# Two boundaries of a decoder layer: the first two tiles of an output product's tail by all tokens instead of by halves

## The chip, the core and the metric

The kernel runs on one core of one Trainium2 chip. The metric is device time in microseconds: the median of several executions of the whole program. Engines are named as in the profile: PE (TensorE) multiplies matrices, PEld is its load of weights, DVE (VectorE) and ACT (ScalarE) work elementwise, POOL is GpSimd, SP issues most DMAs. Each engine works its queue in the order in which instructions were put there, and waits where an input is missing.

## The reference

One decoder layer over 512 tokens of width 1024, in float32, with three residual steps:

```python
h = rms_norm(x, ffn1_pre_g);  x = x + 0.5 * rms_norm(swiglu(h, ffn1_w_in, ffn1_w_out), ffn1_post_g)
h = rms_norm(x, mix_pre_g);   proj = h @ w_mix_in           # q, k, v, u
mixed = concat([dilated_attention(q, k, v), s5_mixer(u, ...)]) @ w_mix_out
x = x + rms_norm(mixed, mix_post_g)
h = rms_norm(x, ffn2_pre_g);  x = x + 0.5 * rms_norm(swiglu(h, ffn2_w_in, ffn2_w_out), ffn2_post_g)

def rms_norm(x, g):   # over the 1024 channels of a token
    return x * rsqrt(mean(x * x) + 1e-6) * g
```

Between two of these steps a *boundary* lies: the output product of the step before has to be finished, its rows normalised and added to `x`, and the new `x`, with the gain of the next norm, goes into the next step's first products. The factor of that next norm is applied later, to the products.

## The kernel before

Activations lie transposed: 128 channels of a tile on the partitions, the 512 tokens along the free dimension; a 1024-wide activation is eight such tiles (`KD` = 8). A token's sum over channels is thus a sum over partitions and over tiles, and is made by matmuls with a column of ones.

Products run in a pair format: an operand is split into a rounded high part and the low rest (`split`: ACT makes `xh`, DVE makes `xl` from `x` and `xh`), and `mm3` issues three matmuls, high by high, high by low, low by high, in this order. A tile of the tail (`NT` = 4 blocks of the inner dimension) is therefore 4 x 3 = 12 matmuls. All matmuls that the boundary issues go through `mm`, which pins them in the order of the program.

`boundary` is called twice: after the first feed-forward step (its output is `y`) and after the mixer (`ymix`). Most of the output product has been made before; what is left is the tail, the last four blocks. The work goes by halves of the tokens (`HT` = 256), so that the norm of the first half can be worked out while TensorE makes the second half:

- `product(h, m)`: the 12 matmuls of output tile m on half h, into half of a PSUM bank; tiles 0 to 5 share a bank by pairs, 6 and 7 have one each.
- `gather(h, m, n, b)` (L287): DVE adds n tiles from PSUM into `y`.
- `squares(h, m, n, eng)` (L293, L296): ACT squares n tiles of `y` and, except for m = 0, which goes straight into `acc[h]`, an addition into `acc[h]` follows, on POOL (`G`) or DVE (`V`). The two columns of `acc[h]` hold even and odd tiles.
- `fold` (L168): POOL adds the two columns of `acc`.
- `post[h][0]`, made by `rstd`: the fold (for the first half), four matmuls `st` with the ones, `nv` on DVE (L190), a power on POOL (L192). `post[h][1]`: four matmuls `rp` that spread the factor over the partitions.
- `prep(h, k)`: L302 and L304 on DVE (scale `y` by the gain and the factor, add to `x`), then `split` for the next step (`xh` on ACT L151, `xl` on DVE L152), and the square of `x` for the next norm (L161, L163 on POOL).
- `begin(h, k)`: 12 matmuls of the next step's first products, into the banks `first`.

Tiles 0 and 1 of the first half come first, the first three blocks of both and then the last block of both, because the last block's input can be late. Then come tiles 2 to 7 of the first half, then the eight tiles of the second half. After tile 2 of the second half stands `post[0][0]`, after tile 3 `post[0][1]` and `prep(0, 0)`, `prep(0, 1)`. Behind the tail the loop over k alternates `prep(0, k)` and `begin(0, k)`; `post[1]` is worked in at k = 2 and 4; then the same for the second half, with the next norm's sums at k = 3 and 6.

The order on an engine is made by a scheduler ahead of time, by a model of readiness and the order of the program. What passes through `fix` is *pinned*: it is issued behind everything that the program has given to that engine before. POOL's additions in `squares` and, where `fixp=fx` is given, POOL's fold and power are pinned. DVE's gathers and the preps up to k = 5 are not.

```python
                (fix if eng is V else fx)(eng.tensor_tensor(out=ac, in0=ac, in1=t, op=ALU.add))   # squares
                self.fold(acc, nc.gpsimd, fixp or fix)                                            # rstd, sums
```

## Time and profile before

| what | value |
|---|---|
| median of 3 runs | 957.33 us (956.88 to 957.65) |
| the profiled execution | 957.78 us, its span 956.0 us |
| granted clock of TensorE, mean | 0.997 |
| first boundary's tail products | 354.66 to 378.13 us |
| its first products of the next step, up to the last spread | 378.13 to 402.40 us |
| second boundary's tail products | 552.54 to 576.60 us |
| its first products of the next step, up to the last spread | 576.60 to 600.90 us |

The span runs from the first to the last instruction. Rows of the timeline give start, length, engine, line, operation, the tile written and those read, shapes and a count, and in brackets how long the engine was idle before and what ended that. A row with a count above 1 is several instructions merged. Rows of the chain of waits give start, length and what the end of the program hung on in that time.

### The profile page before, as it was taken

The numbers are of one execution on the slowest core, as the hardware profiler recorded it, in microseconds if no ns is written. First come the engines' busy times: TensorE is split into PE (matmuls) and PEld (weight loads), VectorE is DVE, ScalarE is ACT, GpSimd is POOL, SyncE is SP. The second block draws the span as 40 slices with busy tenths as digits, with TensorE's granted clock in tenths as the row PEclk, the third lists the DMA queues.
The fourth block names the chain that finished last, engine by engine and source line by source line (L and its number), as shares of the span: only waits on it lengthen the run. The fifth ranks groups of instructions, "written<-read, shape, count | busy, mean of one in ns | idle before, by whom it ended". The sixth has DMA issues, their size and how long they took to land.

```text
span 956.0 us, 12871 instructions
## 1 busy us (share of the span) xinstructions
PE 942.2 (99%) x5082; PEld 789.3 (83%) x5082; DVE 528.3 (55%) x934; ACT 367.3 (38%) x610; POOL 223.5 (23%) x134
## 2 busy tenths in 40 slices
PE   9999999999999999999999999999999999999995
PEld 7888888888888889978777899888888888888884
DVE  6999213463256546758897659644135524453427
ACT  6354334352234233525646645543233222232312
POOL 0234222322223233500000034421112112223300
PEclk9999999999999999999999999999999999999998
DMA  8223334353334241292323420422232222323202
GB/s 264 90 99 109 102 110 138 125 177 103 106 114 132 67 154 45 90 232 81 121 71 126 147 90 1 131 79 99 88 111 89 93 105 89 110 88 132 88 1 89
DMA packets 38173, 102.48 MB, mean 107 GB/s; under 512 B 7616, under 2 KB 10944, under 8 KB 37568
## 3 DMA queue, kind: packets, MB, share of 16 engines
q1 hardware_dynamic: 36528, 98.02, 31.8%
q10 hardware_dynamic: 1584, 3.63, 1.1%
q8 instruction: 40, 0.66, 0.3%
q14 instruction: 21, 0.17, 0.1%
HBM read 94.03 MB, written 7.60 MB: 106 GB/s over the span
## 4 chain that ended last, share of the span: by engine, by line
PE 93%; DVE 3%; ACT 1%; issue 1%; DMA 1%; POOLq 0%; POOL 0%; ACTq 0%; DVEq 0%; SPq 0%
PE gu L129 47%; PE yo L129 20%; PE first L129 6%; PE yt L129 6%; PE prj L129 3%; PE prv L129 2%; PE mo L129 2%; PE st L129 1%; PE ys L129 1%; PE gl L129 1%; PE pt L832 1%; PE sc L129 1%; PE pv L129 1%; PE rp L129 0%; ACT whi L102 0%
## 5 line engine op out<-in xcount | busy, mean ns | idle before, releaser
L104 POOL TENSOR_TENSOR wlo<-wraw,whi 128x1024 fp32r<-128x1024 f32 (+2 forms) x62 | 156.6, 2526 | 498.9 <-ACT whi L102 490.7
L102 ACT CAST whi<-wraw 128x1024 fp32r<-128x1024 f32 (+5 forms) x157 | 154.6, 990 | 303.5 <-PE gu L129 119.8
L129 PE MATMUL gu<-xh,whi 128*128 128x512 f32 x656 | 257.7, 393 | 0.0
L129 PE MATMUL gu<-xh,wlo 128*128 128x512 f32 x656 | 255.7, 390 | 0.5 <-DVE wlo L104 0.5
L129 PE MATMUL gu<-xl,whi 128*128 128x512 f32 x656 | 255.3, 389 | 0.0
L104 DVE TENSOR_TENSOR wlo<-wraw,whi 128x1024 fp32r<-128x1024 f32 (+5 forms) x95 | 115.9, 1226 | 121.7 <-ACT whi L102 121.4
L129 PEld LDWEIGHTS gu<-xh,wlo 128*128 128x128 f32 x656 | 123.1, 188 | 27.0 <-DVE wlo L104 1.0
L129 PEld LDWEIGHTS gu<-xh,whi 128*128 128x128 f32 x656 | 123.2, 188 | 25.3 <-issue 0.4
L129 PEld LDWEIGHTS gu<-xl,whi 128*128 128x128 f32 x656 | 123.2, 188 | 25.0
L402 DVE TENSOR_TENSOR ut<-gu,rs 128x512 f32<-128x512 f32 x41 | 28.2, 689 | 102.9 <-PE gu L129 102.9
L149 DVE TENSOR_TENSOR al<-ut,ah 128x512 fp32r<-128x512 f32 x44 | 65.7, 1494 | 25.4 <-ACT ah L148 25.4
L129 PE MATMUL yo<-ah,whi 128*128 128x512 f32 x144 | 56.0, 389 | 0.0
L129 PE MATMUL yo<-al,whi 128*128 128x512 f32 x144 | 56.0, 389 | 0.0
L129 PE MATMUL yo<-whi,ah 128*128 128x512 f32 x144 | 56.0, 389 | 0.0
L129 PE MATMUL yo<-wlo,ah 128*128 128x512 f32 x144 | 56.0, 389 | 0.0
L129 PE MATMUL yo<-whi,al 128*128 128x512 f32 x144 | 56.0, 389 | 0.0
L129 PE MATMUL yo<-ah,wlo 128*128 128x512 f32 x144 | 56.0, 389 | 0.0
L400 DVE TENSOR_TENSOR gt<-gu,rs 128x512 f32<-128x512 f32 x41 | 28.2, 688 | 50.0 <-PE gu L129 50.0
L148 ACT CAST ah<-ut 128x512 fp32r<-128x512 f32 x44 | 27.3, 622 | 64.3 <-DVE ut L403 64.3
L129 PE MATMUL first<-xh,whi 128*128 128x256 f32 (+1 forms) x144 | 44.0, 306 | 0.2 <-ACT xh L151 0.2
L403 DVE TENSOR_TENSOR ut<-ut,gt 128x512 f32<-128x512 f32 x44 | 41.5, 946 | 4.1 <-ACT whi L102 0.5
L129 PE MATMUL first<-xl,whi 128*128 128x256 f32 (+1 forms) x144 | 43.5, 302 | 0.0
(194 smaller groups left out, 1410.2 us busy)
## 6 DMA issues: line engine op xcount, KB each, us to landing
wraw<-w2i SPq DMA_DIRECT2D x44, 512.0 KB, 3.5
wraw<-w1i SPq DMA_DIRECT2D x42, 512.0 KB, 3.5
wraw<-w2o SPq DMA_DIRECT2D x18, 512.0 KB, 3.4
wraw<-w1o SPq DMA_DIRECT2D x16, 448.0 KB, 3.4
wraw<-wmi SPq DMA_DIRECT2D x12, 512.0 KB, 3.6
x<-xT SPq DMA_DIRECT2D x8, 256.0 KB, 4.8
w1d<-w1s SPq DMA_DIRECT2D x8, 256.0 KB, 2.8
w2d<-zb SPq DMA_DIRECT2D x2, 1024.0 KB, 4.9
```

The lines of the kernel that those rows point to most:

```text
L102: fix(self.nc.scalar.copy(out=hi, in_=raw))
L104: fix(eng.tensor_tensor(out=lo, in0=raw, in1=hi.bitcast(F32), op=ALU.subtract))
L129: i = self.nc.tensor.matmul(*a, **k)
L148: fix(nc.scalar.copy(out=hi, in_=src))
L149: fix(nc.vector.tensor_tensor(out=lo, in0=src, in1=hi.bitcast(F32), op=ALU.subtract))
L400: nc.vector.tensor_tensor(out=gt, in0=o[f][0], in1=r, op=ALU.mult)
L402: nc.vector.tensor_tensor(out=ut, in0=o[f][1], in1=r, op=ALU.mult)
L403: nc.vector.tensor_tensor(out=ut, in0=ut, in1=gt, op=ALU.mult)
L832: self.fix(nc.tensor.transpose(b[i][:, o:o + P], sc[:, c:c + P], self.ident))
```

## The change

In `boundary`, tiles 0 and 1 of the tail are made on all 512 tokens, with their own bank each, at the start; the second half's loop begins with tile 2. The gathers of the two tiles are 512 wide, and their squares are taken for both halves at once. The calls of `post[0]` in the second half's loop stand behind tiles 4 and 5 instead of 2 and 3.

```diff
@@ -311,15 +311,16 @@
         V, G, fx = nc.vector, nc.gpsimd, self.fix
-        b2 = [self.bank("yt")[:, :HT] for _ in range(2)]
+        b2 = [self.bank("yt") for _ in range(2)]
         for ks in (range(NT - 1), (NT - 1,)):
             for m in range(2):
                 for k in ks:
                     th, tl = tail(k)
-                    self.mm3(b2[m], tw(0, m, k), tw(1, m, k), th[:, hs[0]], tl[:, hs[0]], k == 0, k == NT - 1)
+                    self.mm3(b2[m], tw(0, m, k), tw(1, m, k), th, tl, k == 0, k == NT - 1)
         for m in range(2):
-            gather(0, m, 1, b2[m].unsqueeze(1))
-        squares(0, 0, 2, V)
+            nc.vector.tensor_tensor(out=y(m), in0=b2[m], in1=y(m), op=ALU.add)
+        for h in range(2):
+            squares(h, 0, 2, V)
         for m in range(2, KD):
             b = product(0, m)
             if m % 2 or m > 5:
@@ -327,7 +328,7 @@
                 gather(0, m, n, b)
                 squares(0, m, n, G if m == 2 else V)
         late = []
-        for m in range(KD):
+        for m in range(2, KD):
             b = product(1, m)
             if m % 2 or m > 5:
                 m1, n = (m - 1, 2) if m < 6 else (m, 1)
@@ -337,9 +338,9 @@
                     late.append(t)
                 if m == 5:
                     self.fold(acc[1], G, fx)
-            if m == 2:
+            if m == 4:
                 post[0][0](fixp=fx)
-            if m == 3:
+            if m == 5:
                 rr[0] = post[0][1]()
                 for k in range(2):
                     prep(0, k)
```

## The prediction

> **What bounds the kernel now.** I read the page first, then the busy time by stretches of the two boundaries, then the chain of waits through them, then the timeline of each engine around the places that the edit moves.

> ```profile
> span 956.0 us, 12871 instructions
> PE 942.2 (99%) x5082; PEld 789.3 (83%) x5082; DVE 528.3 (55%) x934; ACT 367.3 (38%) x610; POOL 223.5 (23%) x134
> 354.66:378.13 23.47, 23.47 (x203) 23.47 (x202) 11.78 (x23) 7.20 (x13) 7.42 (x6) 1.00 0.18 62
> 552.54:576.60 24.06, 23.73 (x203) 23.53 (x202) 14.10 (x26) 9.08 (x16) 7.49 (x7) 1.00 0.21 67
> ```

> The last two rows are the tail products of the first and of the second boundary; their columns are the stretch and its length, then the busy time of PE, PEld, DVE, ACT and POOL, the granted clock, and the DMA's share and rate. TensorE is busy in all of the first tail and misses 0.33 us in the second, at a granted clock of 1.00. So nothing but TensorE's own time can be saved there, and any wait of TensorE that the edit makes is added to the span one for one. Whether there is such a wait is the whole question.

> ```profile
> 333.06 21.76 PE yo L129 x96
> 354.82 15.55 PE yt L129 x132
> 372.67 5.46 PE yt L129 x48
> ...
> 553.81 0.04 issue
> 553.85 14.99 PE yt L129 x125
> 568.85 0.34 PE st L129 x4
> 569.18 1.52 PE yt L129 x12
> 570.70 0.45 PE rp L129 x4
> 571.15 5.46 PE yt L129 x48
> 576.61 4.32 PE first L129 x36
> ```

> These are pieces of the chain of waits (start, length, what). One 512-wide product costs 21.76 / 96 = 0.2267 us, a 256-wide one 15.55 / 132 = 0.1178 us. The order of TensorE around the row sums is to be seen too: products, `st` (sums of the first half's squares), one tile of 12 products, `rp` (the spread of the norm), four more tiles (48 products), then `first`, the next stage's products on the first half.

> **Wider tiles.** The edit takes 48 products of 256 away and puts 24 of 512 in: 48 x 0.1178 - 24 x 0.2267 = 0.21 us less in each boundary, 0.42 us in both. Of the tail's 192 products 144 stay as they are.

> **The start of the second boundary.** Here products wait for the gated SSM outputs (`so`).

> ```profile
> 552.54 0.99 PE L129 MATMUL yt<-so,tw 128*128 128x256 f32 x7
> 553.85 14.99 PE L129 MATMUL yt<-so,tw 128*128 128x256 f32 x125 [0.33 <-DVE so L152]
> 553.12 1.47 DVE L152 SCALAR_TENSOR_TENSOR so<-go,so 128x512 fp32r<-128x512 f32 x2
> ```

> The eighth product needs the low part of the third `so` tile; it would start at 552.54 + 7 x 0.1178 = 553.36 and starts at 553.85, a hole of 0.49 us. With 512-wide products the eighth is due at 552.54 + 7 x 0.2267 = 554.13, after the tile has come, and the last `so` tile (done at 553.12 + 1.47 = 554.59) is wanted only behind 18 products, at 556.6. The hole goes: 0.49 us less. The first boundary has no such hole.

> **The first row sums.** This is the step that I think decides. `post[0][0]` moves from behind tile 2 to behind tile 4 of the second half. It issues one fold of `acc[0]` on POOL (L168), four `st` products, `nv` on DVE and a power on POOL. The fold is pinned in program order (`fixp=fx`), behind whatever POOL got before it. Today the only tile pair of the second half ahead of it is (0, 1), and `squares` issues no addition for m = 0. After the edit the pair (2, 3) is ahead, whose `squares(1, 2, 2, G)` issues a pinned POOL addition of 128x512. So the fold stands in POOL's queue behind an addition whose input comes from products that TensorE has finished only one tile before. The `st` products need the fold, and all matmuls are pinned, so behind the waiting `st` stand product(1, 5), the spread and everything else.

> ```profile
> 558.99 0.69 DVE L287 TENSOR_TENSOR ymix<-yt,ymix 128x512 f32<-128x512 f32 x1 [2.26 <-PE yt L129]
> 559.77 0.63 ACT L293 ACTIVATE sq<-ymix 128x512 f32<-128x512 f32 x1 [2.38 <-DVE ymix L287]
> 560.48 1.28 POOL L296 TENSOR_TENSOR acc<-acc,sq 128x512 f32<-128x512 f32 x1 [1.78 <-ACT sq L293]
> 565.25 0.78 DVE L296 TENSOR_TENSOR acc<-acc,sq 128x256 f32<-128x256 f32 x2 [0.19 <-ACT sq L293]
> 566.12 0.74 POOL L168 TENSOR_TENSOR acc<-acc 128x256 f32<-128x256 f32 x1 [4.35 <-DVE acc L296]
> 567.47 0.69 DVE L287 TENSOR_TENSOR ymix<-yt,ymix 128x512 f32<-128x512 f32 x1 [1.43 <-PE yt L129]
> 568.57 0.53 PEld L129 LDWEIGHTS st<-ones,acc 128*128 128x128 f32 x4
> ```

> The first three rows are the same kind of pair (tiles 2 and 3 of the first half): from the gather's start to the POOL addition's start 560.48 - 558.99 = 1.49 us, the addition 1.28. The fold today starts 566.12 - 566.03 = 0.09 us after what it waits for and takes 0.74; TensorE picks up a finished input in about 0.04 us (553.81, where the DVE op before it in the chain ends, to 553.85). So `st` can load 1.49 + 1.28 + 0.09 + 0.74 + 0.04 = 3.64 us after the start of the gather of (2, 3). TensorE is ready for it one tile after that pair, and the last two rows show that distance for the pair (0, 1) today: 568.57 - 567.47 = 1.10 us. **The wait is 3.64 - 1.10 = 2.54 us in each boundary, 5.08 us in both.** Today's slack hides nothing of it: the fold ends at 566.86 and `st` comes at 568.57, 1.7 us of cover, and that cover is what the queue position takes away. Below and above: no wait if the fold were issued ahead of the addition, 2.54 as derived, and up to 0.19 more if the addition takes 1.47 as in a row below. I take 2.54.

> The chance to do better, that POOL overtakes, has no row in this trace. [...]

> **The spread to the first products.** `rp` ended at 571.15, and 48 products (5.46 us) lay between it and `first`. After the edit only tiles 6 and 7 lie there, 24 x 0.1178 = 2.83 us. In that time `prep(0, 0)` must deliver `xh` and `xl`.

> ```profile
> 571.35 0.86 DVE L302 SCALAR_TENSOR_TENSOR ymix<-ymix,sm,rp 128x256 f32<-128x256 f32 x2
> 572.13 1.85 DVE L304 TENSOR_TENSOR x<-ymix,x 128x256 f32<-128x256 f32 x2
> 573.91 0.47 DVE L302 SCALAR_TENSOR_TENSOR ymix<-ymix,sm,rp 128x256 f32<-128x256 f32 x1
> 574.30 0.48 DVE L152 SCALAR_TENSOR_TENSOR xl<-x,sm,xh 128x256 fp32r<-128x256 f32 x1
> 572.24 1.47 POOL L296 TENSOR_TENSOR acc<-acc,sq 128x512 f32<-128x512 f32 x1 [2.07 <-ACT sq L293]
> 572.58 0.51 ACT L151 ACTIVATE xh<-x,sm 128x256 fp32r<-128x256 f32 x1 [0.42 <-DVE x L304]
> 375.82 0.47 DVE L152 SCALAR_TENSOR_TENSOR xl<-x,sm,xh 128x256 fp32r<-128x256 f32 x1
> 576.91 0.41 DVE L287 TENSOR_TENSOR ymix<-yt,ymix 128x256 f32<-128x256 f32 x1
> ```

> The first `xl` is there at 574.30 + 0.48 = 574.78, 3.63 us after `rp` ended at 571.15 (in the first boundary at 376.29, 3.62 us after its `rp` ended at 372.67). The second `first` product needs it, at 2.83 + 0.12 = 2.95 us. With 0.04 us to pick it up: **0.72 us of wait in each boundary, 1.44 in both.** I expect the same order on DVE and the same POOL addition beside it, now that of the pair (4, 5), so the same 3.63. Bounds: if DVE's order puts the low part directly behind the long L304 (573.98), 0.40 us less; if two 256-wide gathers (0.41 each) slip in, 0.82 more. So 0.32 to 1.54.

> **The rest of the prepared half.** Behind the spread `first` stands 5.46 - 2.83 - 0.72 = 1.91 us nearer to `rp` than today, so later preps have less time.

> ```profile
> 574.69 0.41 DVE L304 TENSOR_TENSOR x<-ymix,x 128x256 f32<-128x256 f32 x1
> 575.91 0.68 DVE L287 TENSOR_TENSOR ymix<-yt,ymix 128x512 f32<-128x512 f32 x1
> 578.02 1.02 DVE L304 TENSOR_TENSOR x<-ymix,x 128x256 f32<-128x256 f32 x1
> 588.57 0.57 DVE L152 SCALAR_TENSOR_TENSOR xl<-x,sm,xh 128x256 fp32r<-128x256 f32 x1
> 585.58 10.08 PE first L129 x84
> ```

> The tightest place is the first `xl` of the second half: done at 589.14, that is 17.99 us behind `rp`, wanted today at 585.58 + 37 x 0.12 = 590.02 (18.87). After the edit it is wanted at 18.87 - 1.91 = 16.96. But DVE has less to do by then: the gather of (4, 5), 0.68, is done before `rp`, and one of the POOL additions that stretch an L304 is gone (1.02 against 0.41 where nothing is beside it, 0.61). 17.99 - 1.29 = 16.70, just in time. I take nothing; the other end, with no such saving, is 17.99 - 16.96 = 1.03 us per boundary. Weight loads, the SP queue, `late` and the second spread keep their places relative to `first`; the end of the boundary hangs on TensorE's own `rp` and moves with it.

> **The sum.** -0.42 - 0.49 + 5.08 + 1.44 = +5.6 us. Against the profiled execution (957.78 us, 956.0 of it span) that is 963.4; it lies 0.45 above the median of the three runs, 957.33, so I forecast **962.9 us** for the median.

> **The rivals.**
> 1. *Only the second wait comes*: the fold is not held, because it is issued ahead of the addition. -0.42 - 0.49 + 1.44 = +0.5, 957.9 us, within what can be told apart: the case on the other side. Place: POOL between tiles 3 and 4 of the second half; it decides if gather to `st` shrinks from 3.64 below 1.10 us. Against it: the pin and the order of the calls. 8%.
> 2. *Neither wait comes*: 957.33 - 0.91 = 956.4 us. It needs also the first `xl` within 2.95 us of `rp`; today it takes 3.63. 4%.
> 3. *Only the first wait comes*: DVE's order brings the low part in time. 962.9 - 1.44 = 961.5 us. 8%.
> 4. *DVE becomes the bound in the second half*: 1.03 us more in each boundary, 965.0 us. For it: a margin of only 0.26 us. 10%.
> 5. *The fold keeps DVE out as well.* The L304 rows show DVE standing still beside POOL: its second L304 ends at 573.98, 0.27 after the POOL addition's end at 573.71. After the edit a fold of 0.74 stands right behind that addition. If POOL holds on for both, `xl` comes 0.83 us later, 962.9 + 1.66 = 964.6 us. 5%. [...] A row speaks against a second op being waited out:

> ```profile
> 577.46 1.30 POOL L296 TENSOR_TENSOR acc<-acc,sq 128x512 f32<-128x512 f32 x1 [1.75 <-ACT sq L293]
> 578.85 0.80 POOL L168 TENSOR_TENSOR acc<-acc 128x256 f32<-128x256 f32 x1
> ```

> The L304 begun at 578.02 ended at 579.04, inside the fold that stood behind the addition: it got in between the two.

> **How the numbers follow.** Forecast 65%, rivals 8, 4, 8, 10 and 5%. The unknown costs alone give 957.33 - 0.91 + 5.08 + 2 x 0.32 = 962.1 to 957.33 - 0.91 + 5.08 + 2 x 1.54 = 964.6; with rival 3 below and 4 above, and some tenths for the scatter of the runs (956.88 to 957.65), **961.0 to 965.3**. Outside are rivals 1 and 2. A measurement of this kernel tells about 0.2%, 1.9 us, from no change: slower means above 959.2. Rivals 1 and 2 fall within: same 0.12; slower 0.85; faster 0.03 for something that I don't see.

> **What would show it.** Right: in both boundaries the POOL fold L168 directly behind an L296 addition, a hole of 2.5 us on TensorE ahead of `st` laid to that fold, a second of 0.7 us ahead of the second `first` product laid to `xl`, and no hole at 553.4. Wrong: a fold that starts before the (2, 3) addition of its half, or TensorE without a hole in the tail; then the sum falls to that of rival 1 or 2. A hole at the start of the second half of `first` is rival 4.

## The result, and the profile after

| | before | changed |
|---|---|---|
| median | 957.29 us (956.88 to 957.65, 4 runs) | 967.30 us (966.29 to 968.62, 4 runs) |
| ratio to before, 95% interval | | 1.0104 [1.0092, 1.0115] |
| profiled execution, its span | 957.78 us, 956.0 us | 966.29 us, 964.5 us |

The changed kernel is 10.0 us slower. The direction was forecast; the size was not: 5.6 us were forecast, and the time lies 2.0 us above the range.

The first fence is from the page of the changed kernel, the second from its waits of TensorE (total us, times, longest).

```profile
span 964.5 us, 12769 instructions
PE 942.9 (98%) x5034; PEld 787.6 (82%) x5034; DVE 526.0 (55%) x932; ACT 367.4 (38%) x610; POOL 227.1 (24%) x134
```

```profile
PE st L129 <- POOL acc L168: 4.2, 2, 2.1
PE first L129 <- DVE xl L152: 2.0, 4, 0.8
PE ys L129 <- issue: 1.8, 2, 0.9
```

TensorE is as busy as before (942.9 against 942.2 us, in a span 8.5 us longer), so the time went into waits. Two of the three rows are the forecast ones: `st` waits for POOL's fold once in each boundary, and `first` waits for `xl`. The third was not forecast; `ys` belongs to the mixer, between the two boundaries.

The chain of waits through the first boundary (start, length, what):

```profile
353.54 16.92 PE yt L129 x120
...
370.48 0.70 DVE y L287
...
371.27 0.64 ACT sq L293
...
371.98 1.26 POOL acc L296
373.24 0.69 POOL acc L168
...
373.98 0.61 PE st L129 x4
374.58 1.49 PE yt L129 x12
...
376.10 0.69 DVE y L287
376.79 0.78 DVE y L302 x2
377.57 1.77 DVE x L304 x2
379.34 0.33 DVE y L287
379.68 0.54 DVE xl L152
...
380.26 4.52 PE first L129 x35
```

Before, this chain held TensorE alone. Now it leaves TensorE twice. First from the gather of tiles (2, 3) over the square and POOL's addition to the fold, which starts the moment the addition ends. Then over DVE from the gather of (4, 5) to the first `xl`, with a gather (L287, 0.33) that stands ahead of `xl`.

To see where each microsecond went, I took the starts of TensorE's first row of each tile from the timeline, in this and every later profile, and their differences as stage lengths, in us:

| stage | before | changed | difference |
|---|---|---|---|
| start of the program, up to the first `rp` | 36.10 | 34.73 | -1.37 |
| first boundary: first `yt` to `st` | 15.55 | 20.60 | +5.05 |
| `st` to `rp` | 1.86 | 1.92 | +0.06 |
| `rp` to `first` | 5.90 | 3.27 | -2.63 |
| `first` to the next stage | 25.82 | 27.13 | +1.31 |
| *first boundary, sum* | 49.13 | 52.92 | +3.79 |
| `ys`, in the mixer | 11.76 | 13.03 | +1.27 |
| second boundary: first `yt` to `st` | 16.14 | 20.59 | +4.45 |
| `st` to `rp` | 1.86 | 3.20 | +1.34 |
| `rp` to `first` | 5.90 | 3.50 | -2.40 |
| `first` to the next stage | 25.83 | 27.08 | +1.25 |
| *second boundary, sum* | 49.73 | 54.37 | +4.64 |

The rest of the span differs by 0.2 us in all. The start is scatter: over the kernels below that leave it alone it lies between 34.5 and 36.1. So the boundaries cost 8.4 us, and `ys` 1.3.

The second boundary holds something that the first does not. Its chain:

```profile
577.05 0.63 PE st L129 x4
577.69 2.77 PE yt L129 x12
580.46 0.74 PE rp L129 x4
```

Twelve products took 2.77 us here and 1.49 in the first boundary, behind the same wait. Busy time by stretches (length, then PE, PEld, DVE, ACT, POOL with counts, granted clock, DMA share and rate), the first boundary in the first two rows and the second in the others:

```profile
369.29:372.70 3.41, 2.57 (x22) 2.36 (x21) 0.69 (x1) 0.63 (x1) 0.72 (x1) 1.00 0.00 0
372.70:376.11 3.41, 2.13 (x18) 2.13 (x19) 0.17 (x2) 0.00 (x0) 1.94 (x3) 1.00 0.02 5
574.09:577.50 3.41, 1.29 (x12) 1.09 (x11) 0.17 (x1) 0.63 (x1) 1.95 (x2) 1.00 0.00 0
577.50:580.91 3.41, 3.41 (x18) 3.41 (x18) 0.57 (x2) 0.00 (x0) 0.71 (x1) 0.50 0.00 0
580.91:584.32 3.41, 3.12 (x27) 2.92 (x26) 3.38 (x7) 1.86 (x4) 2.19 (x2) 1.00 0.03 7
```

The granted clock fell to 0.50 for 3.41 us behind the wait of the second boundary and stayed at 1.00 behind that of the first; why the stretches are cut at these times is told with e10. Against the first boundary's lengths the lower clock cost 3.20 - 1.92 + 3.50 - 3.27 = 1.51 us.

### The profile page after: what moved, and what is told of

Same layout as the page of the kernel before. It is cut to its first block, busy times and chain, and to the rows that moved or that the text cites. A ratio compares the mean times of both kernels' runs of the same rounds, so it can differ in the third digit from the quotient of the medians.

```text
span 964.5 us, 12769 instructions
## 1 busy us (share of the span) xinstructions
PE 942.9 (98%) x5034; PEld 787.6 (82%) x5034; DVE 526.0 (55%) x932; ACT 367.4 (38%) x610; POOL 227.1 (24%) x134
## 3 DMA queue, kind: packets, MB, share of 16 engines
q10 hardware_dynamic: 1584, 3.63, 1.1%
## 4 chain that ended last, share of the span: by engine, by line
PE 90%; DVE 5%; DMA 1%; issue 1%; ACT 1%; POOL 1%; POOLq 0%; DVEq 0%; ACTq 0%
PE gu L129 45%; PE yo L129 20%; PE yt L129 5%; PE first L129 5%; PE prj L129 3%; PE mo L129 2%; PE prv L129 2%; PE st L129 1%; PE ys L129 1%; PE gl L129 1%; DMA wraw<-w1i 1%; DVE wlo L104 1%; PE pt L833 1%; PE sc L129 1%; PE pv L129 1%
## 5 line engine op out<-in xcount | busy, mean ns | idle before, releaser
L129 PE MATMUL gu<-xh,whi 128*128 128x512 f32 x656 | 257.6, 393 | 0.0
L129 PE MATMUL gu<-xh,wlo 128*128 128x512 f32 x656 | 255.7, 390 | 0.5 <-DVE wlo L104 0.5
L129 PE MATMUL gu<-xl,whi 128*128 128x512 f32 x656 | 255.3, 389 | 0.0
L129 PEld LDWEIGHTS gu<-xh,wlo 128*128 128x128 f32 x656 | 123.1, 188 | 26.8 <-DVE wlo L104 1.0
L129 PEld LDWEIGHTS gu<-xh,whi 128*128 128x128 f32 x656 | 123.2, 188 | 25.3 <-issue 0.4
L129 PEld LDWEIGHTS gu<-xl,whi 128*128 128x128 f32 x656 | 123.2, 188 | 25.1
L149 DVE TENSOR_TENSOR al<-ut,ah 128x512 fp32r<-128x512 f32 x44 | 68.6, 1560 | 25.4 <-ACT ah L148 25.4
L129 PE MATMUL yo<-ah,whi 128*128 128x512 f32 x144 | 56.0, 389 | 0.0
L129 PE MATMUL yo<-al,whi 128*128 128x512 f32 x144 | 56.0, 389 | 0.0
L129 PE MATMUL yo<-whi,ah 128*128 128x512 f32 x144 | 56.0, 389 | 0.0
L129 PE MATMUL yo<-wlo,ah 128*128 128x512 f32 x144 | 56.0, 389 | 0.0
L129 PE MATMUL yo<-whi,al 128*128 128x512 f32 x144 | 56.0, 389 | 0.0
L129 PE MATMUL yo<-ah,wlo 128*128 128x512 f32 x144 | 56.0, 389 | 0.0
L129 PE MATMUL first<-xl,whi 128*128 128x256 f32 (+1 forms) x144 | 43.2, 300 | 2.0 <-DVE xl L152 2.0
L129 PE MATMUL first<-xh,whi 128*128 128x256 f32 (+1 forms) x144 | 43.2, 300 | 0.8 <-ACT xh L151 0.8
L129 PE MATMUL first<-xh,wlo 128*128 128x256 f32 (+1 forms) x144 | 42.4, 295 | 0.0
```

The lines of the kernel that those rows point to most:

```text
L129: i = self.nc.tensor.matmul(*a, **k)
L149: fix(nc.vector.tensor_tensor(out=lo, in0=src, in1=hi.bitcast(F32), op=ALU.subtract))
```

## The experiments

Each kernel is the changed kernel with the edit shown, unless another is named. The ratios are to runs of the kernel before beside it (medians 957.21, 957.14 and 956.82 us in the three groups of runs). In the expectations A is the theory that POOL's and DVE's queues make the waits and that TensorE, idle in them, then gets a lower clock; the theory called F is explained where it comes up, and the rivals B, C, D, G and H in the expectations that name them.

### The wait at `st`

**e1: the fold ahead of the second half.** It is issued before the loop, so that no addition stands ahead of it.

```diff
-        def sums(more=(), fix=lambda i: i, fixp=None):
+        def sums(more=(), fix=lambda i: i, fixp=None, fold=True):
-            if folded and not more:
+            if fold and folded and not more:
...
         late = []
+        self.fold(acc[0], G, fx)
         for m in range(2, KD):
...
-                post[0][0](fixp=fx)
+                post[0][0](fixp=fx, fold=False)
```

> The changed kernel with one difference: the fold of acc[0] is issued on POOL ahead of the second half's additions; st, nv and the power stay where the change put them. Theory A (POOL's order holds st, and the idle TensorE then gets a lower clock): st waits for nothing; the power, pinned behind the addition of tiles 2 and 3, comes 0.6 us late, so rp waits 0.6 us per boundary; the granted clock is back at 0.997; the wait at the second first product stays at 1.0. Time 957.3 - 0.9 + 2 x 0.6 + 2 x 1.2 = 960 us, between 959 and 961.5. Rival B (st waits for its late place and for gathers that come late, whatever POOL's order): st still waits over 2 us, time 966 to 968.

964.04 us (960.94 to 965.03), ratio 1.0067 [1.0053, 1.0081]. The chain of the first boundary:

```profile
371.64 1.28 POOL acc L296
372.92 0.69 POOL p L192
...
373.66 0.72 PE rp L129 x4
```

The wait at `st` is gone from both boundaries (first `yt` to `st` 18.33 us in place of 20.60). The power (L192), now the op behind the addition, comes late in place of the fold, and `rp` waits a little: `st` to `rp` is 2.29, against 1.86 where nothing is late. So POOL's order makes the wait. The time is 4 us above the 960 that A expected, though, and 2.5 above its range: `ys` took 15.69 us in this profile.

**e2: that addition on DVE.**

```diff
-                t = squares(1, m1, n, G if n == 2 else None)
+                t = squares(1, m1, n, (V if m1 == 2 else G) if n == 2 else None)
```

> The changed kernel with one difference: the addition of the squares of tiles 2 and 3 of the second half runs on DVE instead of POOL, so nothing stands ahead of the fold in POOL's queue. Theory A: no wait at st nor at rp, clock back at 0.997, what is left is the second wait of about 1.2 us per boundary. Time 957.3 - 0.9 + 2.4 = 958.8 us, between 957.8 and 960. Rival B: st still waits over 2 us, 966 to 968.

963.40 us (962.02 to 964.55), ratio 1.0065 [1.0052, 1.0077]. Both boundaries now take 50.58 us, with 18.33 to `st` and 1.85 from there to `rp`: no wait at `st`, none at `rp`, and no fall of the clock in either. The difference to the changed kernel, 20.60 - 18.33 = 2.27 us, is what the first wait costs in a boundary, lower clock not counted. The `xl` wait stayed (27.12). And again the time is above A, which expected 958.8, again by `ys`: 16.40 us.

**e3 and e10: work put into the wait, and behind it.** Twenty spare products of 128x256 into an unused bank stand ahead of `st` in e3, and behind it in e10.

```diff
             if m == 4:
+                fill = self.bank("idle")
+                for _ in range(20):
+                    self.mm(fill[:, :HT], lhsT=tw(0, 0, 0), rhs=tail(0)[0][:, hs[0]], start=True, stop=True)
                 post[0][0](fixp=fx)
```

> The changed kernel with 20 more matmuls of 128x256 into a spare bank directly ahead of st, work that nothing reads: they fill the wait (20 x 0.118 = 2.4 us) and take no time from anything else if st has to wait 2.5 us anyway. Theory A (the idle 2.3 us lowers TensorE's clock afterwards): the clock stays at 0.997 and the time falls by what the lower clock cost, to 964 us, between 963 and 965.5, with less spread between runs. Rival C (the surplus over the forecast has nothing to do with the clock): 967.3 as before, or slower.

> The changed kernel with the same 20 spare matmuls of 128x256, now behind st instead of ahead of it: TensorE idles through the wait as in the changed kernel and then has 2.4 us more to do, where the filler ahead of st filled the wait. Both kernels issue the same instructions. Theory A (an idle of 2.3 us lowers the granted clock for some us afterwards): slower than the kernel with the filler ahead by 2.4 us per boundary and by what the lower clock costs, 1 to 2 us where it falls: 965.0 + 4.7 + 2 to 4 = 972 to 974, granted clock 0.99 or below, windows behind st at 0.5 to 0.9. Rival C (no clock effect): 965.0 + 4.7 = 969.7 and the clock at 0.996.

e3: 964.98 us (963.82 to 966.18), ratio 1.0080 [1.0067, 1.0093]. e10: 972.44 us (970.83 to 973.07), ratio 1.0155 [1.0135, 1.0175]. Chains of the first boundary, e3 and then e10:

```profile
372.74 2.35 PE idle L129 x20
375.09 0.40 PE st L129 x4
375.50 1.50 PE yt L129 x12
```

```profile
374.30 0.61 PE st L129 x4
374.91 3.99 PE idle L129 x20
378.90 1.37 PE yt L129 x12
```

In e3 the 2.35 us of spare work cost nothing: `st` comes 20.68 us after the first `yt`, against 20.60 without them. They lie wholly within the wait. In e10 the same products cost their full time, and more, because they run at the lower clock: 3.99 us in place of 2.35. Stretches of e10:

```profile
374.00:376.00 2.00, 1.70 (x11) 1.70 (x12) 0.16 (x1) 0.00 (x0) 0.97 (x2) 0.76 0.03 8
376.00:378.00 2.00, 2.00 (x11) 2.00 (x11) 0.00 (x0) 0.00 (x0) 0.00 (x0) 0.50 0.00 0
378.00:380.00 2.00, 2.00 (x18) 2.00 (x18) 0.00 (x0) 0.00 (x0) 0.00 (x0) 0.89 0.00 0
```

In e3, where TensorE does not stand idle there, the boundaries' clock stayed at 1.00 (353 to 382 us and 555 to 586 us). So it was the idle stretch that the clock fell behind, and e3 is faster than the changed kernel though it does more work. e3 and e10 issue the same instructions, and only the order differs: 972.44 - 964.98 = 7.46 us between the medians, of which the 40 spare products at full clock explain 4.70. The other 2.8 come with the lower clock, in the median and not only in one profile: the four executions of e10 had mean granted clocks of 0.992 to 0.995, the six of e3 0.996 to 0.998.

Some of what decides whether the clock falls behind a wait can be read off the times at which it fell. e6, an experiment told below, has the same two waits, and its clock fell in both boundaries:

```profile
378.48:381.89 3.41, 3.41 (x17) 3.41 (x17) 0.85 (x2) 0.00 (x0) 0.72 (x1) 0.50 0.00 0
583.28:586.69 3.41, 3.41 (x19) 3.41 (x18) 1.98 (x4) 0.63 (x1) 0.81 (x2) 0.50 0.01 2
```

The two falls are 583.28 - 378.48 = 204.80 us apart, 60 x 3.413. e10's are as far apart (375.04 and 579.84). In the changed kernel the clock changed at 577.50 and 580.91, 3.41 us apart, and fell again at 956.38, when the products were done, 375.47 us or 110 x 3.413 later. So within each of these three profiles the times lie on a grid of 3.41 us, and the grid's place is not the same in all: 583.28 in e6 and 577.50 in the changed kernel are 5.78 us apart, 1.7 stretches. In the changed kernel the second wait (574.94 to 577.06) lies whole in one stretch, 574.09 to 577.50, and the next stretch is at half clock. The first wait (371.86 to 373.98) is cut by the line at 372.70 (577.50 less 60 stretches) into 0.84 and 1.28 us, and the clock stays. Four profiles have two such waits each, of 2.12 to 2.17 us: changed, e6, e10 and e12. In e6 and e10 each wait has 2.05 us or more within the one stretch ahead of a fall. In e12, where the clock is 0.60 from 376 to 378 us and 0.54 from 378 to 380, the fall began at about 376.4; the first wait (373.32 to 375.44) lies whole in the stretch ahead of it, and the second (576.62 to 578.79) is cut at about 577.8 and was followed by a clock of 1.00 (580 to 582). So six of the eight were followed by a fall, and the two that were not are the two that the grid cut into pieces of 1.3 us or less.

Other stretches agree with this. At the changed kernel's end one with 2.01 us of idle time (952.97 to 956.38) was followed by a fall. The waits of 2.25, 2.56 and 3.35 us in `ys` in e1, e4 and e2, told below, have matmuls of 35 ns behind them in place of 29; behind e8's wait of 1.57 us there they take 29. How much idle time it takes between 1.57 and 2.01 us is not shown. A fall in a boundary lasted one stretch, in e10's second boundary two; one stretch at half clock loses 3.41 / 2 = 1.7 us of work.

### The wait for `xl`, and DVE's order

**e4: the sums and the spread early.** `post[0][0]` directly behind tile 3's products and ahead of the gather of (2, 3); the spread and two preps behind tile 4.

```diff
             b = product(1, m)
+            if m == 3:
+                post[0][0](fixp=fx)
             if m % 2 or m > 5:
...
             if m == 4:
-                post[0][0](fixp=fx)
-            if m == 5:
                 rr[0] = post[0][1]()
```

> The wide tiles of the change, but the sums st and the fold are issued behind product 3 and ahead of the gather and the squares of tiles 2 and 3, the spread rp behind product 4, with three tiles left behind it. Theory A: the fold is done 2.2 us after the first half's last product and st comes after 2.8, no wait; behind rp lie 36 products, 4.2 us, more than the 3.7 that the first xl needs, no wait; what is left is the gain of wide tiles and of the hole at the start of the second boundary, -0.9 us: 956.4 us, between 955.9 and 957.2. Rival D (DVE is the bound of what follows, since TensorE comes 1.2 us earlier): waits at later first products, 957.5 to 959. Rival B: over 960.

959.64 us (955.57 to 962.40, 12 runs), ratio 1.0025 [1.0013, 1.0037]. The boundaries fell to 49.54 and 49.52 us. `st` no longer waits. A wait of 0.3 us is left in each boundary, at the third `first` tile, for its `xl`, which stands on DVE behind gathers and two L302 (26.17 in place of 25.82). A had expected 956.4. `ys` was 15.58 us in this profile, in which the mean granted clock was 0.995. Three of the twelve executions were at 0.995; the other nine, at 0.996 or 0.997, have a median of 959.2, so a fall of the clock is not all that keeps e4 above the kernel before.

**e9: that prep earlier.** On top of e4 and of the shift explained below, `prep(0, 2)` is called with the first two.

```diff
-                for k in range(2):
+                for k in range(3):
                     prep(0, k)
         for k in range(KD):
-            if k > 1:
+            if k > 2:
                 prep(0, k, fx if k > 5 else lambda i: i)
```

> The shifted kernel with the early sums and with prep(0, 2) called beside prep(0, 0) and prep(0, 1), so that DVE is given it ahead of the last gathers. In the early-sums kernel TensorE waits 0.8 us per boundary at the third first product for DVE's order (gathers of tiles 6 and 7 and two L302 ahead). If that order is the cause, the waits at first go from 1.6 us in all to under 0.6 and the time is about 1 us below that of the shifted early-sums kernel, 955.5; if DVE is simply full there, the wait moves to a later first product or to the second half's sums and the time stays.

960.92 us (959.83 to 961.69), ratio 1.0040 [1.0028, 1.0053]. `first` to the next stage is back at 25.83 us in both boundaries, as before the change; DVE's order was the cause. Against e7, which differs from it by this prep alone, the boundaries are 0.49 us shorter and the median 0.49 (960.92 against 961.41).

### The third place: `ys`

e1, e2 and e4, in which the wait at `st` is taken away, kept several microseconds that the boundaries did not hold. In their profiles they were in `ys`, 384 matmuls of about 30 ns with a load each. Its code is the same in all kernels. Chains of before, changed and e2, in this order (e4's is like e2's, its wait 2.56):

```profile
523.01 6.46 PE ys L129 x229
529.48 0.74 issue
530.22 4.56 PE ys L129 x155
```

```profile
525.68 0.36 PE ys L129 x8
526.03 0.93 issue
526.96 6.97 PE ys L129 x246
533.93 0.91 issue
534.84 3.87 PE ys L129 x130
```

```profile
524.86 3.48 PE ys L129 x118
528.34 3.35 issue
531.69 9.03 PE ys L129 x258
```

"Issue" is time whose end the chain lays to no other engine. It lay behind matmul 229 of the stage before the change, and behind 8, 126 (8 + 118) or 254 (8 + 246) after it. Behind the longest of these waits the rest of the stage also ran at 35 ns a matmul (9.03 / 258, in e1 and e4 as in e2) in place of 29 (4.56 / 155); in the stretch 519 to 541 the granted clock is 0.92 in e2 and e4, and 1.00 before and after the change.

The wait behind 8 has an input that was late. The ninth matmul is the first that reads `w`, which four DMAs fill (L125). The first of them was issued at 518.18 before and at 520.84 after the change, and took until it landed, before and then changed:

```profile
DMA to landing us min/median/max: 4.8/4.8/4.8
```

```profile
DMA to landing us min/median/max: 5.9/5.9/5.9
```

It landed at 522.98 and at 526.77. The ninth matmul starts 0.2 us behind that landing in both (at 523.19 and 526.96): before the change that was just when TensorE came to it, after it 0.93 us late. In e1 to e4, e6, e7, e9, e11 and e13 a wait stands behind 8 as well, of 0.15 to 0.72 us. The rest of this section is on the other wait, the one that moves.

Theory F is my assumption, on which the next runs were laid out: TensorE's instructions come in blocks, and a block that is late beside bulk transfers stops TensorE; where in the stage the blocks begin depends on how many instructions came before. The change takes 24 matmuls with 24 loads away in the first boundary, 48 instructions, and by F moves that place. What speaks for blocks are packets of a queue of their own on the page, in before 0.66 MB in 40, each of 16,384 bytes in the trace:

```profile
q8 instruction: 40, 0.66, 0.3%
```

**e6, e7, e8: the place put back, or moved, from the start.** Five warm-up products at the start become two, and 15 tiny ones come behind: 12 more matmuls in the program's text, which the page counts as 24 (5058 in e6, 5034 in the changed kernel), with 24 loads; the five warm-up products of before likewise stand in its trace as 10 matmuls and 10 loads. e6 is the changed kernel with it (the places of before again), e7 is e4 with it, e8 is the kernel before with it (moved the other way).

```diff
-        for _ in range(5):
+        for _ in range(2):
             self.mm(idle[:, :HT], lhsT=warm[:, :P], rhs=warm, start=True, stop=True)
+        for _ in range(15):
+            self.mm(idle[:, :2], lhsT=warm[:, :P], rhs=warm[:, :2], start=True, stop=True)
```

> The changed kernel; of the five warm-up matmuls at its start three are left out and 15 tiny ones (128x2, of two passes each) put in, so that 24 more matmuls and 24 more weight loads lie ahead of everything: as many as the change took away ahead of the mixer. TensorE's instruction stream then stands where it stood in the kernel before when the outputs of the SSM (ys) begin. Theory F (the instruction fetch is late at ys, and how late hangs on where the stream's blocks of 16 KB begin): the wait laid to issue in ys falls to the 0.7 us of the kernel before, the stage ys to 11.8 us, and the time falls from 967.3 to about 964, what the two waits and the clock in the boundaries cost. Rival G (the wait in ys varies from run to run whatever the position): no change that the interval shows, 966 to 968.

> The kernel with the early sums, with the same shift of TensorE's instruction stream. Theory F: the stage ys falls from 15.6 to 11.8 us, no lower clock behind it, the time from 959.6 to about 956.5 (956 to 957.3), with the spread of the kernel before. Rival G: 959 to 960 and runs from 956 to 962 as without the shift.

> The kernel before with the same shift at its start, as a control. It shows what the swap of the warm-up matmuls costs by itself (at most 0.5 us by the start of the first products), and moves the stream by 48 instructions away from where it stood. Theory F: the wait in ys changes in place and size, by 22 to 24 matmuls earlier, and may grow by up to 3 us; Rival G: wait and time as before, 957.2.

e6: 970.63 us (969.88 to 970.91), ratio 1.0141 [1.0127, 1.0155]. e7: 961.41 (961.07 to 962.32), 1.0050 [1.0036, 1.0063]. e8: 961.58 (959.49 to 963.04), 1.0048 [1.0035, 1.0061]. As times these runs missed, since the edit has a price of its own that I had put at half a microsecond at most: the first `rp` came at 38.4 to 38.7 us, 2.3 to 2.6 later than before. e6 moreover shows the lower clock in both boundaries (54.83 and 54.18 us). The profiles do tell the theories apart. `ys` fell from 13.03 to 12.15 us with e6, of which the wait for `w` makes 0.25, and from 15.58 to 12.47 with e7; the other wait stands behind 230 (8 + 222) in both, and in e9, e11 and e13, which have such a shift too. And in e8 the wait of the unchanged code moved:

```profile
525.38 0.36 PE ys L131 x8
...
525.75 5.65 PE ys L131 x197
531.40 1.57 issue
532.97 5.21 PE ys L131 x179
```

It stands behind 205 matmuls (8 + 197), 24 fewer than before (229), as many as were put in ahead. In e3, which has 20 matmuls more than the changed kernel at that point, 4 fewer than before, it stands behind 8 + 226 = 234. So this wait moved with the number of instructions ahead of it, by 24 matmuls for 24 in e8 and by 5 for 4 in e3, while the program of `ys` stayed the same.

The DMA records of the traces fit a late block as well. In the four profiles read for it, a packet of the instruction queue (16,384 bytes) ended 1.4 to 1.5 us before TensorE went on: from 527.68 to 528.78 before the change, where TensorE went on at 530.22; from 532.34 to 533.37 and 534.84 in the changed kernel; from 529.40 to 530.31 and 531.69 in e2; from 530.42 to 531.45 and 532.97 in e8. e10 has no such wait: there the packet ended at 535.37, and matmul 234 was not due before 537.2. But the place does not set the length. The changed kernel passes 126 without a wait, and its packet (525.91 to 526.89) came 0.3 us behind the first load of `ys`; e1, e2 and e4 wait at 126, for 2.25 to 3.35 us, and there it came 4.1 to 5.2 us behind it. What held it up in them is not shown.

**e12: a cheaper shift on the changed kernel** (the tiny products 2x2 in place of 128x2).

```diff
+        for _ in range(15):
+            self.mm(idle[:2, :2], lhsT=warm[:, :2], rhs=warm[:, :2], start=True, stop=True)
```

> The changed kernel with the same cheap shift: the same two waits and the same lower clock in the boundaries, but ys where the kernel before had it. Theory F (position of the instruction stream): ys in 11.8 to 12.5 us, 964.5 to 966.5 us, below the 967.3 of the changed kernel. Rival G: 967.3.

967.70 us (966.56 to 969.06), ratio 1.0109 [1.0089, 1.0129]. `ys` was 12.15 us, as F said, and yet the median is that of the changed kernel, which is what the rival G said. In the profiles the start takes back what `ys` brought: the first `rp` comes at 36.31 us, 0.2 later than before the change but 1.6 later than in the changed kernel, and the clock fell once in each. For the size of F in the median this run says nothing, and against it if anything.

### What is left of the wide tiles

**e11: e9 with the cheap shift**, without the two waits and with the instructions in the places of before.

> The wide tiles with early sums and prep(0, 2) pulled ahead, and the shift of TensorE's stream by 15 tiny matmuls of two weight columns each (2x2) in place of three warm-up matmuls. The wider tiny ones took the start of the second stage of products from 37.2 to 40.7 us; these should leave it at 37 to 38. From the profile of the slower variant (959.9 us of span, 3.5 late at the start) the time should be 957.5 us, between 956 and 958.5: the gain of the wide tiles is then at most some tenths, since in the profile they take 0.233 us per matmul and two halves 2 x 0.1174.

957.94 us (956.73 to 959.31, 12 runs), ratio 1.0006 [0.9997, 1.0016]. Both boundaries together are 0.35 us below before (49.19 and 49.32), `ys` 1.09 above. This is the best version with wide tiles, and no difference from the kernel before can be measured.

**e13: wide tiles with `post[0]` where it was**, and the cheap shift.

```diff
-            if m == 4:
+            if m == 2:
                 post[0][0](fixp=fx)
-            if m == 5:
+            if m == 3:
                 rr[0] = post[0][1]()
```

> The wide tiles alone: post[0] stays behind tiles 2 and 3 of the second half as in the kernel before, with the cheap shift. Ahead of st lie then only 12 products of the second half instead of 36; the fold is done 2.2 us after the first half's last product and st is reached after 1.4, so a wait of about 0.85 us per boundary at st by theory A, none at the first products (48 products lie behind rp), and no lower clock: 957.2 + 1.7 - 0.5 = 958.4, between 957.5 and 959.5. If the wide tiles themselves were at fault (rival H), most of the 10 us would stay: over 963.

959.74 us (958.79 to 961.88, 12 runs), ratio 1.0028 [1.0017, 1.0038]. With the loop starting at tile 2 the sums stand one tile, 1.4 us, behind the first half's last product. The fold needs that product's gather, its square and an addition on DVE first, and is done 2.2 us behind it (369.20 to 371.38 in the first boundary), so `st` waits:

```profile
PE st L131 <- POOL acc L170: 1.7, 2, 0.9
```

No wait for `xl`, no lower clock: the time is 0.2 us above the range that A gave. So moving `post[0]` later was not needed for the wide tiles, and earlier (e11) is better than either.

### All runs together

Differences to before, in us: boundaries and `ys` from the one profile of each, the start likewise, and the median.

| kernel | both boundaries | `ys` | start | median |
|---|---|---|---|---|
| changed | +8.4 | +1.3 | -1.4 | +10.0 |
| e1 fold first | +3.8 | +3.9 | -1.6 | +6.8 |
| e2 addition on DVE | +2.3 | +4.6 | -0.3 | +6.2 |
| e3 spare work in the wait | +7.1 | +0.3 | -0.5 | +7.8 |
| e10 spare work behind it | +16.4 | -0.3 | -1.0 | +15.6 |
| e4 early sums | +0.2 | +3.8 | -1.4 | +2.4 |
| e6 changed, shifted | +10.2 | +0.4 | +2.6 | +13.5 |
| e7 e4, shifted | +0.2 | +0.7 | +2.4 | +4.3 |
| e8 before, shifted | 0.0 | +1.0 | +2.3 | +4.4 |
| e9 e7 and earlier prep | -0.3 | +0.4 | +3.6 | +3.8 |
| e12 changed, cheap shift | +8.2 | +0.4 | +0.2 | +10.9 |
| e13 old places, cheap shift | +1.5 | +0.3 | +0.3 | +2.9 |
| e11 e9, cheap shift | -0.35 | +1.1 | 0.0 | +1.1 |

The three columns add up to the median within 2.1 us everywhere. They come from one execution each, and the fall of the clock, `ys` and the start differ from one execution to the next. The largest gap, e12's, is such a one.

## Why the prediction was right in direction and too small

- **What bounds the kernel** held: TensorE is on the path in the tails, and each of its waits was added to the span.
- **The first wait** came as derived, from the place in POOL's queue (e1, e2, e3 and e10 each show it by another way): 2.27 us in a boundary where 2.54 was forecast, 4.54 in place of 5.08 in both. That the fold does not pass the addition had no row in the profile before; the changed kernel has them: in the first boundary the last addition into `acc[0]` was done on DVE at 369.00, yet POOL stood idle on to 371.98, took the addition of the pair (2, 3), and began the fold at 373.20. From the gather's start to `st` it took 373.98 - 370.48 = 3.50 us (3.64 forecast: the fold was 0.69 long, not 0.74, and stood without a gap). TensorE was ready 12 products after 370.46, so at 371.87, 1.39 us after the gather began; I had read 1.10 off the weight load, which comes ahead of its matmul.
- **The second wait** came with `xl` as its cause: 1.31 and 1.25 us where 0.72 was forecast, 2.56 in place of 1.44 in both, within the bounds of 0.32 to 1.54 for each. One 256-wide gather slipped in ahead of `xl`, which I had held as half of the upper bound. The wait's rows give 2.0 us of it, four waits and not two; the rest is that the products behind it run at 129 ns (4.52 / 35) in place of 120 (3.96 / 33).
- **Wider tiles** brought nothing: -0.42 us was forecast. A wide product takes (16.92 - 96 x 0.1178) / 24 = 0.234 us in the tail, not the 0.2267 of `yo`, which leaves 0.04 us in a boundary. From the first `yt` to `first` it took 23.31 us before and 23.37 in e4 and e11, which have no wait there.
- **The hole** at the start of the second boundary went: 16.14 against 15.55 us before, both 20.6 after; 0.59 in place of 0.49.
- **The rest of the prepared half**, taken as nothing with little margin, held: e9 and e11 have no wait at the second half, and what `first` lost in the changed kernel it lost at its first tiles.
- **The rivals**: 1, 2 and 3, in which one or both waits stay away, are out, and so are 4 (DVE as the bound later) and 5 (the fold keeping DVE out): the two L304 beside POOL's addition took 1.86 and 1.87 us in the two boundaries, where 1.85 was read before, and were done at 379.35 and 583.88, while the fold behind the addition ran (379.13 to 379.92 and 583.67 to 584.47).

**The step that failed** is the sum, -0.42 - 0.49 + 5.08 + 1.44, in which each wait cost only its own length, with TensorE's clock at 1.00 behind it. Its terms were mis-sized: tail and hole brought 0.29 where 0.91 was forecast (e2's length to `first` against before's: 23.46 - 23.31 in the first boundary, 23.46 - 23.90 in the second), the first wait cost 4.54 where 5.08 was forecast, the second 2.56 where 1.44 was. Together that is 6.8 in place of 5.6; it alone would have been 964.1 us, within the range, and that errors of 0.62, -0.54 and 1.12 come to no more is in part luck. What took the time out of the range are costs that the sum did not have. The first is the granted clock, which I quoted as 1.00 and used as a state of affairs. It fell to 0.50 behind six of the eight waits of this length: 1.5 us in the profiled execution, where it came in one boundary, 3.2 in e6, where it came in both (54.83 + 54.18 against twice the 52.92 of the first boundary), and 4.7 in e10, where one of the two falls was twice as long. e3 against e10 shows it in the medians too. The second stands outside the boundaries: `ys` was 1.3 us longer in the profiled execution. Of that 0.9 is the later landing of `w` and 0.2 the longer wait at the moved place (0.91 against 0.74); that the edit brought the late landing about is not shown, and it does not hang on the shift, since in e6, with the places of before, TensorE still waits 0.68 us for `w`. 6.8 + 1.5 + 1.3 = 9.6 of the 10.0 measured between the medians; between the two profiled executions it is 8.5, since in the changed kernel's the start happened to be 1.4 us shorter.

**What stays open.** That late blocks of instructions stop `ys` behind 126, 205, 229, 230, 234 or 254 fits the places and the packets' times, and is otherwise not shown; why a block comes late, and that the bulk of other transfers beside it is the reason, was not tried by itself. How much of the median is due to `ys` was not isolated: in e12 the place was put back and the median did not fall. How often the clock falls in the executions that were not profiled is not known; the four of the changed kernel had mean granted clocks of 0.994 (the profiled one), 0.993, 0.993 and 0.992.

## What to carry to other kernels

Before a step is moved behind other work, read for each engine that it uses what is pinned ahead of it at the new place: a fold of 0.7 us with 1.7 us of cover became the end of the path because one addition of 1.3 us came to stand ahead of it. A wait of 2 us on TensorE is to be priced with what may follow it at half clock, here up to 1.7 us for each wait and in one case twice that; work that has to be done anyway, or even spare work, is free inside it (e3's 2.35 us moved `st` by 0.08). Where a difference lies in a stage that the edit does not touch, compare the stages' lengths one by one. Then look at each stop for what the next instruction reads and when that landed, and only then count the instructions that were taken away ahead of it, before a theory of the edit is stretched to cover it.
